# Rooms for the side jobs in a four-layer trunk: the operators' temporary gets its full size, the phases' tables leave the weight buffers

## The chip, the cores and the metric

One Trainium2 chip, one core in use. The metric is the device time of one execution in microseconds; of several runs the median counts. Profiles are of one execution.

## The reference

The model is a trunk of four layers on 512 tokens of width 1024, in f32. Each layer adds a mixer (S5, gated linear attention, differential attention, S5 again) and a feed-forward to the residual x:

```python
h = rmsnorm(x, norm_mix[layer])
x = x + mix(h)
h = rmsnorm(x, norm_ffn[layer])
g, u = split(h @ w_gate_up)            # 1024 -> 2 x 2816
x = x + (silu(g) * u) @ w_down         # 2816 -> 1024
```

The S5 mixer's recurrence over the sequence is linear with a constant complex diagonal: bb = f * b, p_j = exp(lr dt j) (cos(li dt j) + i sin(li dt j)), y = Re(c s) + d h. Its small operators (products of b, c and powers of the diagonal, and the cosine and sine of the phases) depend only on the weights of that layer, not on x.

## The kernel before

**Matmuls.** Products are f32 in three pieces: a weight tile is cast to a high part (ScalarE, L348) and a low part (VectorE, L356), and three matmuls (L376 to L378 for the down projection) add high by high, high by low and low by high. The gate and up products go by blocks of 256 hidden columns with seven products in place of eight (`seven_block`, matmuls of L543 into banks a, c, d), for which weight quarters are summed: by an accumulating DMA on POOL's queue (L579, "accum") and by VectorE (L636). Weight quarters sit in rotating slots ("slot", "halves", "gain", "side" are the names of such rooms). High and low parts share five buffers ("whl"), raw weights three ("wst").

**A pass.** A feed-forward has eleven blocks, in passes of 3, 3, 3, 2 in layer 0 and of 4, 4, 3 in the others. Behind a pass come its down products, `gemm_b`, for the left half of the output columns (d = 0) and then for the right (d = 1), each with four accumulator banks, one per 128 tokens; L526 adds a finished bank to x. The next half or the next block takes up a bank when L526 has read it.

**Jobs.** Beside the down products of two feed-forwards, `gemm_b` steps a generator once for each 128-row piece and token tile (`self.job()`, L403). What it yields comes between matmuls, so its vector and scalar work is placed there in each engine's own stream. In layer 0 the generator is `s5_spilled`: for the last layer's S5 it makes, in eight groups, the input operators X (`s5_x`), the output operators Q (`s5_q`), small transposes and maps (TensorE tiles xps, rps, cps), and stores them to DRAM ("in", "out", "map"). X is made by `cross`, a product pair with a temporary of tag "dx", Q by the same with the temporary "dq". X's last three powers need 192 elements of dx (L1070), the first needs 64. In layer 1 the generator is first the small tables of the attention, and then `s5_phases_spilled`: eight groups of angles, clamped, and their sine and cosine, each stored to DRAM as "cs".

**Rooms.** The jobs of layer 0 take their tiles from `Slices`, which hands out stretches of two large tiles one behind the other; the size of a tag's stretch is fixed by its first request, and a later, larger request of the tag starts at the same place. dx is first asked for with 64 elements, Q (tag "Q") is asked for next. In layer 1 each group of phases takes one whl buffer (8 KB a partition) for its angles g1 and its two tables cs. The names lie in the trace as "halves" (the rooms of layer 0's jobs) and "phases".

**Order.** Each engine runs its own instructions in the order of its stream, which a scheduler fixes when the kernel is built; between engines semaphores order what shares a room. DMAs issued on one queue go out in that order: SP's has the raw weights, POOL's the accumulating loads and all loads and stores of the jobs.

Of the kernel before, what the change touches and what calls it, by code (L numbers as in the profile page):

```python
# [11 lines left out]
F32 = mybir.dt.float32  # L12
# [3 lines left out]
AF = mybir.ActivationFunctionType  # L16
# [5 lines left out]
P = 128  # L22
# [246 lines left out]
class Trunk:  # L269
# [425 lines left out]
    def ffn(self, l, left, after=None, turn=False, aside=None, small=None):  # L695
# [7 lines left out]
        with self.tc.tile_pool(name=f"ffn{l}", bufs=1, reuse_waits="tile") as fp:  # L703

            na = 3 if aside else 4
            room = lambda: fp.tile([P, 2, 4, 256], F32, tag="act", name="lent", bufs=na)
# [5 lines left out]
            slots = [fp.tile([P, 4, 256], F32, name=f"slot{n}") for n in range(SLOTS + 2 * (4 - na))]  # L712
# [31 lines left out]
            for step in plan.split():  # L744
                name, _, n = step.partition(":")
# [18 lines left out]
            F = left.freed()  # L764
            if aside:

                self.jobs = aside(Slices(left.whole, left.g))
            else:

                self.jobs = small() if small else iter(())  # L770
                slots[:] = [F[0], F[1], slots[0], F[2], left.g[:].rearrange("p (k n) -> p k n", n=256), F[3]] + slots[1:]
            b0 = 0
            for nb in (4, 4, 3) if na == 4 else (3, 3, 3, 2):
                acts = []
                for n in range(b0, b0 + nb):
                    b = blocks[n]
# [450 lines left out]
            r = slice(g * 64, (g + 1) * 64)  # L1227
            self.nc.scalar.copy(d[r, :, :, r], ps[r])

    def s5_phases(self, pool, tag, L, kk, cs):  # L1230

        nc = self.nc
        v = nc.vector
        c = slice(L * NB + 4 * kk, L * NB + 4 * kk + 4)
        g1 = pool.tile([P, 4, P], F32, tag=tag, name="g")
        g2 = cs[:, 0].rearrange("p (b m) -> p b m", b=4)
        col = lambda k, b: self.k5[k][:, c.start + b : c.start + b + 1]
        for b in range(4):
            nc.scalar.activation(g2[:, b], self.mrow[:], AF.Identity, scale=col("f", b), bias=self.magic[:])
        yield  # L1240
        v.tensor_scalar_add(g2, g2, -MAGIC)
        yield
        for b in range(4):
            v.scalar_tensor_tensor(g1[:, b], self.mrow[:], col("fhi", b), g2[:, b], op0=ALU.mult, op1=ALU.subtract)
            v.scalar_tensor_tensor(g1[:, b], self.mrow[:], col("flo", b), g1[:, b], op0=ALU.mult, op1=ALU.add)
            yield
        v.tensor_scalar(g1, g1, -0.5, 0.5, op0=ALU.max, op1=ALU.min)
        yield
        ca = g1.rearrange("p b m -> p (b m)")
        nc.scalar.activation(cs[:, 1], ca, AF.Sin, scale=self.two_pi)  # L1250
        nc.scalar.activation(ca, ca, AF.Abs)
        nc.scalar.activation(cs[:, 0], ca, AF.Sin, scale=-self.two_pi, bias=self.halfpi[:])

    def s5_b_pads(self, bp, X, copies=False):
        for z in range(2):
# [6 lines left out]
    def s5_spilled(self, pool, L):  # L1262


        nc = self.nc
        inm = pool.tile([P, 2, 4, 64], F32, name="inmsp")
        mp = pool.tile([P, 4, 64], F32, name="mapsp")
        bp = pool.tile([P, 2, P], F32, name="bpsp")
        rs = pool.tile([P, 1, 112], F32, name="rssp")
        self.zero_off(bp, 16)  # L1270
        nc.gpsimd.memset(rs[:, :, :48], 0.0)
        self.spill = [{} for _ in range(8)]
        self.dq = nc.gpsimd
        raw = self.s5_loads(pool, L, 0, 4)

        def diag(dst, ps):
            for g in range(2):
                r = slice(g * 64, (g + 1) * 64)
                nc.scalar.copy(dst[r], ps[r, :, r])

        for kk in range(8):
            bb, craw = raw
            yield
            ps = self.s5_qt(craw)
            X, pre, one, two = self.s5_x(nc.vector, pool, L, 4 * kk, 4, bb)
            pre()
            one()
            yield
            yield
            two()  # L1290
            Q, base, one, two = self.s5_q(nc.vector, pool, L, 4 * kk, 4)
            base(ps)
            yield
            yield
            one()
            self.s5_b_pads(bp, X, True)
            yield
            yield
            two()
            if kk < 7:  # L1300
                raw = self.s5_loads(pool, L, 4 * kk + 4, 4)
            yield
            yield
            x0 = self.s5_xt(X, 0, 0)
            yield
            yield
            diag(inm[:, 0], x0)
            yield
            yield
            rv = self.s5_rows(4, bp, Q)  # L1310
            yield
            x1 = self.s5_xt(X, 1, 0)
            yield
            self.s5_map(L, 4 * kk, 4, rv, rs, mp, True)
            yield
            diag(inm[:, 1], x1)
            d = {w: self.dp.tile([P, n], F32, name=f"{w}{kk}") for w, n in (("in", 512), ("out", 512), ("map", 256))}
            nc.gpsimd.dma_start(d["in"][:], inm.rearrange("p a b c -> p (a b c)"))
            nc.gpsimd.dma_start(d["out"][:].rearrange("p (z b n) -> p z b n", z=2, b=4), Q[:, :, :, 1:5].rearrange("p z b j h -> p z b (j h)"))
            nc.gpsimd.dma_start(d["map"][:], mp.rearrange("p b n -> p (b n)"))  # L1320
            self.spill[kk].update(d)
            yield

    def s5_phases_spilled(self, L):

        for kk in range(8):
            p = Slices(self.wp.tile([P, 2048], F32, tag="whl", name="phases", bufs=5))
            cs = p.tile([P, 2, 512], F32, name="cssp")
            yield from self.s5_phases(p, "gsp", L, kk, cs)
            d = self.spill[kk]["cs"] = self.dp.tile([P, 1024], F32, name=f"cs{kk}")  # L1330
            self.nc.gpsimd.dma_start(d[:], cs.rearrange("p a b -> p (a b)"))
            for _ in range(4):
                yield

    def s5_in(self, p, xin, behind=()):
# [1113 lines left out]
```

## Time and profile before

| | |
|---|---|
| Median of 3 runs | 2328.56 us (2325.9 to 2330.97) |
| Span of the profiled execution | 2331.1 us |
| TensorE busy | 2227.3 us, 96% |
| VectorE busy | 1592.5 us, 68% |
| ScalarE busy | 1107.0 us, 47% |
| POOL busy | 276.6 us, 12% |
| Moved by DMA | 319.91 MB, mean 137 GB/s |

The profile's page gives no time of its execution but the span; it lies 0.1 above the slowest of the three runs and 2.5 above their median. A row of a timeline has the start in us, the duration, the engine, the line, the operation, what is written and read, and in brackets the idle time ahead of it with what ended that idle time. A row of waits has the sum, the number and the longest. Waits of an engine that is not the bound cost nothing by themselves. The granted clock of TensorE is a share of its full clock.

### The profile page before, as it was taken

The numbers are of one execution on the slowest core, as the hardware profiler recorded it, in microseconds if no ns is written. First come the engines' busy times: TensorE is split into PE (matmuls) and PEld (weight loads), VectorE is DVE, ScalarE is ACT, GpSimd is POOL, SyncE is SP. The second block draws the span as 40 slices with busy tenths as digits, with TensorE's granted clock in tenths as the row PEclk, the third lists the DMA queues.
The fourth block names the chain that finished last, engine by engine and source line by source line (L and its number), as shares of the span: only waits on it lengthen the run. The fifth ranks groups of instructions, "written<-read, shape, count | busy, mean of one in ns | idle before, by whom it ended". The sixth has DMA issues, their size and how long they took to land. (4 is left out here: it accounts for less than half of the span.)

```text
span 2331.1 us, 37161 instructions
## 1 busy us (share of the span) xinstructions
PE 2227.3 (96%) x14847; PEld 1975.7 (85%) x14847; DVE 1592.5 (68%) x2461; ACT 1107.0 (47%) x1769; POOL 276.6 (12%) x378
## 2 busy tenths in 40 slices
PE   5889989999999999999999998999999899999997
PEld 3778979898877799898988787989999788989996
DVE  8874877777624478786754676876766864967674
ACT  5533645454452355555534675653534233634342
POOL 1000132513000011110002131111000100101000
PEclk8899999999999999999999999999999999999999
DMA  4246566665322358675345465886641556766531
GB/s 85 40 125 180 140 156 161 157 171 135 109 89 73 115 140 204 166 170 168 86 146 128 108 132 144 207 215 146 164 117 54 133 150 151 191 172 159 159 81 64
DMA packets 295719, 319.91 MB, mean 137 GB/s; under 512 B 72125, under 2 KB 235225, under 8 KB 295290
## 3 DMA queue, kind: packets, MB, share of 16 engines
q1 hardware_dynamic: 233434, 236.31, 33.9%
q0 software_dynamic: 62112, 81.22, 18.7%
q8 instruction: 117, 1.92, 0.3%
q14 instruction: 56, 0.46, 0.1%
HBM read 285.62 MB, written 16.65 MB: 130 GB/s over the span
## 5 line engine op out<-in xcount | busy, mean ns | idle before, releaser
L356 DVE TENSOR_TENSOR whl<-wst,whl 128x1024 fp32r<-128x1024 f32 x272 | 331.3, 1223 | 255.1 <-ACT whl L348 254.6
L348 ACT CAST whl<-wst 128x1024 fp32r<-128x1024 f32 x272 | 284.3, 1051 | 319.0 <-PE acc L378 231.6
L543 PE MATMUL a<-side,whl 128*128 128x256 f32 x3168 | 384.0, 277 | 11.2 <-DVE whl L356 6.0
L543 PEld LDWEIGHTS a<-side,whl 128*128 128x128 f32 x3168 | 371.4, 188 | 13.0 <-DVE whl L356 6.8
L376 PE MATMUL acc<-whl,act 128*128 128x512 f32 x704 | 278.8, 396 | 0.0
L377 PE MATMUL acc<-whl,act 128*128 128x512 f32 x704 | 275.7, 392 | 0.0
L378 PE MATMUL acc<-whl,act 128*128 128x512 f32 x704 | 275.4, 391 | 0.0
L543 PE MATMUL c<-side,whl 128*128 128x256 f32 x2112 | 254.7, 277 | 2.9 <-DVE whl L356 2.9
L543 PEld LDWEIGHTS c<-side,whl 128*128 128x128 f32 x2112 | 247.2, 188 | 3.7 <-DVE whl L356 3.7
L356 DVE TENSOR_TENSOR whl<-slot,whl 128x1024 fp32r<-128x1024 f32 x105 | 127.9, 1223 | 68.5 <-ACT whl L348 68.4
L376 PEld LDWEIGHTS acc<-whl,act 128*128 128x128 f32 x704 | 132.7, 188 | 29.2 <-issue 1.2
L378 PEld LDWEIGHTS acc<-whl,act 128*128 128x128 f32 x704 | 132.7, 189 | 28.1
L377 PEld LDWEIGHTS acc<-whl,act 128*128 128x128 f32 x704 | 132.8, 189 | 26.1
L348 ACT CAST whl<-slot 128x1024 fp32r<-128x1024 f32 x105 | 110.1, 1054 | 80.5 <-PE acc L378 34.5
L376 PE MATMUL acc<-whl,hT 128*128 128x512 f32 x352 | 142.7, 405 | 2.1 <-DVE ro L2174 1.5
L543 PE MATMUL a<-sides,whl 128*128 128x256 f32 x1056 | 136.6, 286 | 2.7 <-DVE x L526 2.7
L377 PE MATMUL acc<-whl,hT 128*128 128x512 f32 x352 | 138.0, 392 | 0.9 <-DVE whl L356 0.9
L378 PE MATMUL acc<-whl,hT 128*128 128x512 f32 x352 | 138.2, 393 | 0.0
L543 PE MATMUL d<-sides,whl 128*128 128x256 f32 x1056 | 134.0, 283 | 1.5 <-ACT whl L348 1.5
L543 PEld LDWEIGHTS a<-sides,whl 128*128 128x128 f32 x1056 | 131.8, 194 | 3.9 <-issue 3.1
L543 PEld LDWEIGHTS d<-sides,whl 128*128 128x128 f32 x1056 | 129.1, 191 | 2.4 <-ACT whl L348 2.4
L682 ACT CAST act<-r 128x512 fp32r<-128x512 f32 (+1 forms) x110 | 66.3, 645 | 116.4 <-DVE r L661 102.9
(448 smaller groups left out, 3905.0 us busy)
## 6 DMA issues: line engine op xcount, KB each, us to landing
wst<-in_ffn_w_gate_up_dram SPq DMA_DIRECT2D x88, 512.0 KB, 4.6
wst<-in_ffn_w_down_dram SPq DMA_DIRECT2D x88, 512.0 KB, 4.5
slot<-in_ffn_w_gate_up_dram SPq DMA_DIRECT2D x69, 512.0 KB, 6.4
wst<-in_ffn_w_gate_up_dram POOLq DMA_DIRECT2D x44, 512.0 KB, 6.1
halves<-in_ffn_w_gate_up_dram SPq DMA_DIRECT2D x42, 512.0 KB, 5.4
wst<-in_s_w_glu_dram SPq DMA_DIRECT2D x32, 512.0 KB, 4.6
wst<-in_gla_w_in_dram SPq DMA_DIRECT2D x24, 512.0 KB, 3.9
wst<-in_diff_w_qkv_dram SPq DMA_DIRECT2D x24, 512.0 KB, 3.7
```

What stands on the lines that cost most here:

```text
L348: self.last["high"] = self.nc.scalar.copy(hl[:, 0], w[:])
L356: self.last["low"] = self.nc.vector.tensor_tensor(hl[:, 1], w[:], hl[:, 0].bitcast(F32), op=ALU.subtract)
L376: mm(out, lh, rh, start=first, stop=False)
L377: mm(out, lh, rl, start=False, stop=False)
L378: self.last["mm"] = mm(out, ll, rh, start=False, stop=last)
L543: mm(o, hl[:, x, k, c], side[:, y, k], start=first and not (j or k or n), stop=k == 3 and n == 2, skip_group_check=True,)
L682: self.last["act high"] = nc.scalar.copy(dst[:, 0, j], src[:, j])
```

## The change

Three edits:

- `s5_spilled` asks for dx once with [P, 4, 3, 16], its largest size, ahead of everything that comes behind it, so later requests of dx lie in 192 elements of their own.
- `s5_phases` takes its angles from a room that is handed in, and its two tables as two separate tiles. The angles lie in the norm's gain tile of the feed-forward (1024 elements a partition, two rooms of 512, group by group in turn). The tables are two tiles of 512 from the pool of normed rows, tag "hh" for even groups, "h" for odd ones, each with two buffers: so the tables of a group take the rooms of the group before the last. The gain tile was one of the rotating weight slots of that feed-forward and is none in layer 1 now: seven slots in place of eight. In layers 2 and 3 nothing changes.
- A group's tables are stored by two DMAs of 256 KB in place of one of 512 KB, and seven turns lie behind a group in place of four.

```diff
--- before.py
+++ after.py
@@ -767,8 +767,11 @@
                 self.jobs = aside(Slices(left.whole, left.g))
             else:
 
-                self.jobs = small() if small else iter(())
-                slots[:] = [F[0], F[1], slots[0], F[2], left.g[:].rearrange("p (k n) -> p k n", n=256), F[3]] + slots[1:]
+                spare = left.g[:].rearrange("p (k n) -> p k n", n=256)
+                slots[:] = [F[0], F[1], slots[0], F[2], *(() if small else (spare,)), F[3]] + slots[1:]
+                if small:
+                    self.turns = left.g[:].rearrange("p (z n) -> p z n", z=2)
+                    self.jobs = small()
             b0 = 0
             for nb in (4, 4, 3) if na == 4 else (3, 3, 3, 2):
                 acts = []
@@ -1227,13 +1230,13 @@
             r = slice(g * 64, (g + 1) * 64)
             self.nc.scalar.copy(d[r, :, :, r], ps[r])
 
-    def s5_phases(self, pool, tag, L, kk, cs):
+    def s5_phases(self, room, L, kk, cs):
 
         nc = self.nc
         v = nc.vector
         c = slice(L * NB + 4 * kk, L * NB + 4 * kk + 4)
-        g1 = pool.tile([P, 4, P], F32, tag=tag, name="g")
-        g2 = cs[:, 0].rearrange("p (b m) -> p b m", b=4)
+        g1 = room.rearrange("p (b m) -> p b m", b=4)
+        g2 = cs[0].rearrange("p (b m) -> p b m", b=4)
         col = lambda k, b: self.k5[k][:, c.start + b : c.start + b + 1]
         for b in range(4):
             nc.scalar.activation(g2[:, b], self.mrow[:], AF.Identity, scale=col("f", b), bias=self.magic[:])
@@ -1247,9 +1250,9 @@
         v.tensor_scalar(g1, g1, -0.5, 0.5, op0=ALU.max, op1=ALU.min)
         yield
         ca = g1.rearrange("p b m -> p (b m)")
-        nc.scalar.activation(cs[:, 1], ca, AF.Sin, scale=self.two_pi)
+        nc.scalar.activation(cs[1], ca, AF.Sin, scale=self.two_pi)
         nc.scalar.activation(ca, ca, AF.Abs)
-        nc.scalar.activation(cs[:, 0], ca, AF.Sin, scale=-self.two_pi, bias=self.halfpi[:])
+        nc.scalar.activation(cs[0], ca, AF.Sin, scale=-self.two_pi, bias=self.halfpi[:])
 
     def s5_b_pads(self, bp, X, copies=False):
         for z in range(2):
@@ -1270,6 +1273,7 @@
         self.zero_off(bp, 16)
         nc.gpsimd.memset(rs[:, :, :48], 0.0)
         self.spill = [{} for _ in range(8)]
+        pool.tile([P, 4, 3, 16], F32, tag="dx", name="dx")
         self.dq = nc.gpsimd
         raw = self.s5_loads(pool, L, 0, 4)
 
@@ -1324,12 +1328,13 @@
     def s5_phases_spilled(self, L):
 
         for kk in range(8):
-            p = Slices(self.wp.tile([P, 2048], F32, tag="whl", name="phases", bufs=5))
-            cs = p.tile([P, 2, 512], F32, name="cssp")
-            yield from self.s5_phases(p, "gsp", L, kk, cs)
+            tag = "h" if kk % 2 else "hh"
+            cs = [self.np_.tile([P, 512], F32, tag=tag, name="cssp", bufs=2)[:] for _ in range(2)]
+            yield from self.s5_phases(self.turns[:, kk % 2], L, kk, cs)
             d = self.spill[kk]["cs"] = self.dp.tile([P, 1024], F32, name=f"cs{kk}")
-            self.nc.gpsimd.dma_start(d[:], cs.rearrange("p a b -> p (a b)"))
-            for _ in range(4):
+            for z in range(2):
+                self.nc.gpsimd.dma_start(d[:, z * 512 : (z + 1) * 512], cs[z])
+            for _ in range(7):
                 yield
 
     def s5_in(self, p, xin, behind=()):
```

Lines from L773 on move by three to five in the changed kernel: L1070 is L1073 there, L1239 is L1242, L1247 is L1250, L1252 is L1255, L1318 and L1319 are L1322 and L1323.

The first place is on VectorE in layer 0, pass 1, at the turn from the first half of the down products to the second (banks acc_2752 to acc_2755). The rows "128x192" of L1070 write dx. Before:

```order
L1069 TENSOR_TENSOR halves_1541<-halves_1541,pw_131 128x4x48
L526 SCALAR_TENSOR_TENSOR x_1537<-acc_2752,rcol_1544,x_1537 128x512
L526 SCALAR_TENSOR_TENSOR x_1537<-acc_2753,rcol_1544,x_1537 128x512
L526 SCALAR_TENSOR_TENSOR x_1537<-acc_2754,rcol_1544,x_1537 128x512
L526 SCALAR_TENSOR_TENSOR x_1537<-acc_2755,rcol_1544,x_1537 128x512
L1070 TENSOR_TENSOR halves_1541<-halves_1541,pw_131 128x192
L1071 TENSOR_TENSOR halves_1541<-halves_1541 128x4x48
L1070 TENSOR_TENSOR halves_1541<-halves_1541,pw_131 128x192
L1071 TENSOR_TENSOR halves_1541<-halves_1541 128x4x48
```

And with the change:

```order
L1073 TENSOR_TENSOR halves_1541<-halves_1541,pw_131 128x192
L1074 TENSOR_TENSOR halves_1541<-halves_1541 128x4x48
L1073 TENSOR_TENSOR halves_1541<-halves_1541,pw_131 128x192
L356 TENSOR_TENSOR whl_3182<-wst_3172,whl_3182 128x1024
L526 SCALAR_TENSOR_TENSOR x_1537<-acc_2752,rcol_1544,x_1537 128x512
L1074 TENSOR_TENSOR halves_1541<-halves_1541 128x4x48
L526 SCALAR_TENSOR_TENSOR x_1537<-acc_2753,rcol_1544,x_1537 128x512
L526 SCALAR_TENSOR_TENSOR x_1537<-acc_2754,rcol_1544,x_1537 128x512
L1072 TENSOR_TENSOR halves_1541<-halves_1541,pw_131 128x4x64
L1073 TENSOR_TENSOR halves_1541<-halves_1541,pw_131 128x256
L526 SCALAR_TENSOR_TENSOR x_1537<-acc_2755,rcol_1544,x_1537 128x512
```

The two products that write dx stand ahead of the four L526 now, and products of Q (128x256, 128x4x64) between the last of them.

The second place is POOL's queue at the same time. in0 and out0 are the stores of the first group, rd1_0 one of its small rows, wst_3178 the accumulating load. Before:

```order
L579 DMA wst_3178<-in_ffn_w_gate_up_dram 128x4x256
L1318 DMA in0_2907<-halves_1541 128x512
L1319 DMA out0_2908<-halves_1541 1024x1x64
L1187 DMA rd1_0_2892<-halves_1541 128x112
L1079 DMA halves_1541<-in_s5_b_im_dram 128x4x16
L1082 DMA halves_1541<-in_s5_c_re_dram 128x64
L1082 DMA halves_1541<-in_s5_c_im_dram 128x64
```

And with the change:

```order
L1082 DMA halves_1541<-in_s5_b_im_dram 128x4x16
L1082 DMA halves_1541<-in_s5_b_re_dram 128x4x16
L1323 DMA out0_2908<-halves_1541 1024x1x64
L1190 DMA rd1_0_2892<-halves_1541 128x112
L1322 DMA in0_2907<-halves_1541 128x512
L1082 DMA halves_1541<-in_s5_b_re_dram 128x4x16
L1082 DMA halves_1541<-in_s5_b_im_dram 128x4x16
```

The store out0 is issued ahead of the loads of the next group, and the accumulating load (L579), which stood in front of it, comes later.

The third place is layer 1, pass 1, the same turn of the down products: ScalarE first. whl_8685 and its like are weights, phases_8576 and cssp_8576 the tables of the first group of phases, phases_8705 and cssp_8732 those of the third. Before:

```order
L1252 ACTIVATE phases_8576<-phases_8576,halfpi_117 128x512
L348 CAST whl_8690<-wst_8688 128x1024
L1250 ACTIVATE phases_8634<-phases_8634 128x512
L1251 ACTIVATE phases_8634<-phases_8634 128x512
L1252 ACTIVATE phases_8634<-phases_8634,halfpi_117 128x512
L1239 ACTIVATE phases_8705<-mrow_232,magic_123,s5f_128 128x128 x4
L348 CAST whl_8731<-wst_8729 128x1024
```

And with the change:

```order
L1253 ACTIVATE cssp_8577<-gain_6967 128x512
L1254 ACTIVATE gain_6967<-gain_6967 128x512
L348 CAST whl_8723<-wst_8721 128x1024
L1255 ACTIVATE cssp_8576<-gain_6967,halfpi_117 128x512
L1242 ACTIVATE cssp_8732<-mrow_232,magic_123,s5f_128 128x128 x4
L348 CAST whl_8768<-wst_8766 128x1024
L1253 ACTIVATE cssp_8646<-gain_6967 128x512
```

The first pieces of the third group stand right behind the last table of the first group now, whose room they write, and a weight's cast behind them; before, a cast and the second group's tables stood between.

VectorE at this turn, acc_8459 to acc_8462 being the banks of the first half. Before:

```order
L356 TENSOR_TENSOR whl_8685<-wst_8683,whl_8685 128x1024
L1247 TENSOR_SCALAR phases_8634<-phases_8634 128x512
L356 TENSOR_TENSOR whl_8690<-wst_8688,whl_8690 128x1024
L526 SCALAR_TENSOR_TENSOR x_1537<-acc_8459,rcol_7149,x_1537 128x512
L526 SCALAR_TENSOR_TENSOR x_1537<-acc_8460,rcol_7149,x_1537 128x512
L526 SCALAR_TENSOR_TENSOR x_1537<-acc_8461,rcol_7149,x_1537 128x512
L526 SCALAR_TENSOR_TENSOR x_1537<-acc_8462,rcol_7149,x_1537 128x512
L1241 TENSOR_SCALAR phases_8705<-phases_8705 128x512
L356 TENSOR_TENSOR whl_8731<-wst_8729,whl_8731 128x1024
```

And with the change:

```order
L1248 SCALAR_TENSOR_TENSOR gain_6967<-mrow_232,s5flo_130,gain_6967 128x128
L1244 TENSOR_SCALAR cssp_8732<-cssp_8732 128x512
L1250 TENSOR_SCALAR gain_6967<-gain_6967 128x512
L1247 SCALAR_TENSOR_TENSOR gain_6967<-mrow_232,s5fhi_129,cssp_8732 128x128 x2
L1248 SCALAR_TENSOR_TENSOR gain_6967<-mrow_232,s5flo_130,gain_6967 128x128 x2
L526 SCALAR_TENSOR_TENSOR x_1537<-acc_8459,rcol_7149,x_1537 128x512
L526 SCALAR_TENSOR_TENSOR x_1537<-acc_8460,rcol_7149,x_1537 128x512
L526 SCALAR_TENSOR_TENSOR x_1537<-acc_8461,rcol_7149,x_1537 128x512
L526 SCALAR_TENSOR_TENSOR x_1537<-acc_8462,rcol_7149,x_1537 128x512
L1247 SCALAR_TENSOR_TENSOR gain_6967<-mrow_232,s5fhi_129,cssp_8732 128x128 x2
L1248 SCALAR_TENSOR_TENSOR gain_6967<-mrow_232,s5flo_130,gain_6967 128x128 x2
L356 TENSOR_TENSOR whl_8768<-wst_8766,whl_8768 128x1024
```

Six instructions on the third group's tables and angles, and the clamp of the second group, stand ahead of the four L526 now; before, the third group began behind them.

## The prediction

> **What bounds the kernel now.** I read the page's busy table first, then the busy times by stretch, then what TensorE waited for, and last the timelines of the engines that it waited for.
>
> ```profile
> PE 2227.3 (96%) x14847; PEld 1975.7 (85%) x14847; DVE 1592.5 (68%) x2461; ACT 1107.0 (47%) x1769; POOL 276.6 (12%) x378
> ...
> 320.00:337.00 17.00, 11.37 (x87) 8.42 (x87) 10.54 (x20) 4.49 (x12) 8.43 (x13) 0.95 0.66 163
> 337.00:345.00 8.00, 8.00 (x58) 5.92 (x56) 5.31 (x16) 3.47 (x10) 2.97 (x6) 0.67 0.49 81
> 430.00:435.00 5.00, 3.76 (x43) 2.74 (x43) 4.57 (x15) 3.13 (x9) 3.17 (x7) 1.00 0.68 181
> 870.00:880.00 10.00, 8.26 (x73) 8.07 (x72) 9.45 (x11) 6.08 (x7) 2.07 (x2) 1.00 1.10 295
> 945.00:968.00 23.00, 23.00 (x104) 18.99 (x102) 14.85 (x38) 11.60 (x20) 2.46 (x4) 1.00 0.56 165
> 968.00:980.00 12.00, 9.27 (x54) 8.95 (x53) 9.50 (x10) 3.78 (x5) 1.31 (x1) 0.72 0.57 131
> ```
>
> In each stretch the columns are its length, then busy time (and count) of PE, PEld, DVE, ACT and POOL, then the granted clock. TensorE is the bound: 96% of the span. So the change can only be worth what it does to the few places where TensorE stands still or runs slowly. It touches two stages: the feed-forward of layer 0 (243 to 620 us), which carries the operators' jobs, and that of layer 1 (850 to 1160 us), which carries the phases' jobs. Where they have no hole, as from 945 to 968, the clock is 1.00 and PE is full.
>
> **Layer 0.** The first hole is in 320 to 337, with a slow clock behind it.
>
> ```profile
> PE xps L1217 <- DVE halves L1071: 4.7, 1, 4.7
> PE rps L1171 <- DVE halves L1069: 1.2, 1, 1.2
> PE rps L1171 <- DVE halves L1071: 0.9, 1, 0.9
> ...
> 336.41 1.12 PE L1217 MATMUL xps<-ident,halves 64*64 64x64 f32 x16 [4.69 <-DVE halves L1071]
> ```
>
> These three waits are all that TensorE's list has for 300 to 620 us. The xps transposes stand in TensorE's stream ahead of the next down products, and wait for a vector product. That one, in turn:
>
> ```profile
> 326.98 2.81 DVE L526 SCALAR_TENSOR_TENSOR x<-acc,rcol,x 128x512 f32<-128x512 f32 x4 [1.60 <-PE acc L378]
> 334.50 0.36 DVE L1070 TENSOR_TENSOR halves<-halves,pw 128x192 f32<-128x192 f32 x1 [4.71 <-DMA out<-halves]
> 335.92 0.35 DVE L1071 TENSOR_TENSOR halves<-halves 128x192 f32<-128x192 f32 x1
> ...
> 323.58 1.31 POOL L579 DMA_DIRECT2D wst<-in_ffn_w_gate_up_dram  x1 [2.83 <-ACT halves L1279]
> 324.37 1.11 POOL L1318 DMA_DIRECT2D in<-halves  x1
> 324.94 1.45 POOL L1319 DMA_DIRECT2D out<-halves  x1
> ...
> out<-halves POOLq DMA_DIRECT2D x1, 256.0 KB, 9.5
> ```
>
> VectorE stood still for 4.71 us in front of L1070, whose output is the 192-element temporary dx, until the store of the previous group's Q had landed: issued at 324.94, plus 9.5, is 334.4. The store was slow because a 512 KB accumulating load (L579) was issued ahead of it on the same queue. A temporary has no reason to wait for that store, except that its room lies on Q's: the code's allocator gave dx 64 elements at its first request and hands out the same start for 192 later.
>
> **Layer 1.** Here the hole is at the turn from the down products of pass 1 to the next block:
>
> ```profile
> 971.08 5.46 PE L543 MATMUL a<-sides,whl 128*128 128x256 f32 x24 [2.73 <-DVE x L526]
> ...
> 966.31 1.22 DVE L356 TENSOR_TENSOR whl<-wst,whl 128x1024 fp32r<-128x1024 f32 x1 [1.64 <-ACT whl L348]
> 967.79 1.22 DVE L356 TENSOR_TENSOR whl<-slot,whl 128x1024 fp32r<-128x1024 f32 x1
> 969.04 1.23 DVE L636 TENSOR_TENSOR slot<-slot,slot 128x1024 f32<-128x1024 f32 x1
> 970.19 2.06 DVE L526 SCALAR_TENSOR_TENSOR x<-acc,rcol,x 128x512 f32<-128x512 f32 x3
> ...
> 965.23 1.05 ACT L348 CAST whl<-wst 128x1024 fp32r<-128x1024 f32 x1 [3.24 <-DMA cs<-phases]
> ...
> 956.41 0.55 POOL L1331 DMA_DIRECT2D cs<-phases  x1 [0.88 <-DVE phases L1244]
> ...
> DMA to landing us min/median/max: 2.9/4.3/8.8
> ```
>
> From the end: TensorE wants the accumulator bank that L526 empties; L526 is queued behind the pieces of three weights; the first of them waits for a cast; and the cast waited 3.24 us for a "whl" buffer that phases held until its store had landed (956.41 + 8.8 = 965.2, the longest of the eight stores). Then the clock falls to 0.72.
>
> **The change part by part.** *dx gets its room.* No instruction is added; the wait of L1070 goes. What is late next: the two 192-element products now stand ahead of the four L526, and out0 is issued ahead of the accumulating load instead of behind it, so the store should land before Q is rewritten. The gain is the 4.69 of idle time and the slow clock behind it: (1 - 0.67) x 8.00 = 2.6. Of the other two waits (0.9 and 1.2 us) the order brings the small matrix products in other places, some of them closer to their inputs: from none to all of 2.1, and I take 1.2. Layer 0: -(4.7 + 2.6 + 1.2) = -8.5, between -7.3 and -9.4 if the store is no longer waited for.
>
> *The phases leave the weight buffers.* All five whl buffers stay with the weights, so the cast at 965.23 needs only TensorE's release of its buffer. The idle 2.73 goes and (1 - 0.72) x 9.27 = 2.6 of slow clock: -5.3. The order has one more L356 and one more L636 ahead of that L526 than before (1.2 us each), but the work can start some 2 us earlier than 966.31; were it not to, 0 to 2.4 us would come back. I take 0.
>
> *gain is no slot.* Seven rotating slots instead of eight in layer 1. Layer 0 has five and its list above has no TensorE wait on a slot: 0. The one load of the norm's gain on SP that now waits for the last angles stands ahead of no block's first weights: 0.
>
> *Rooms of two, and two stores per group.* This is what the change adds: eight more stores, whose issue (0.55 us each on POOL) lies beside everything. But a table room is reused by the group after next, so the first ScalarE piece of group 2 waits until the second half of group 0 has landed. Before, its buffer came round in the same way, but the pieces stood behind the second group's tables, and their vector work behind L526. In the new order they come right behind group 0's last table, and they and their vector work stand ahead of the L526 of the first down half. Before:
>
> ```profile
> 939.49 0.72 ACT L1252 ACTIVATE phases<-phases,halfpi 128x512 f32<-128x512 f32 x1
> ...
> 940.51 0.58 POOL L1331 DMA_DIRECT2D cs<-phases  x1 [23.12 <-DVE phases L1245]
> ...
> 944.10 1.64 ACT L1239 ACTIVATE phases<-mrow,magic,s5f 128x128 f32<-128x128 f32 x4
> ...
> 944.59 2.79 DVE L526 SCALAR_TENSOR_TENSOR x<-acc,rcol,x 128x512 f32<-128x512 f32 x4 [1.09 <-PE acc L378]
> 947.29 0.42 DVE L1241 TENSOR_SCALAR phases<-phases 128x512 f32<-128x512 f32 x1
> 948.86 0.61 DVE L1244 SCALAR_TENSOR_TENSOR phases<-mrow,s5fhi,phases 128x128 f32<-128x128 f32 x2
> ...
> 946.43 0.39 PE L376 MATMUL acc<-whl,act 128*128 128x512 f32 x1
> ```
>
> With group 0 ready at the same time, its second half is issued at about 940.5. Landing takes 2.9 to 4.3 (the shortest and the median of the 512 KB stores; half the bytes, so rather the shorter): 943.4 to 944.8. Then four pieces on ScalarE (1.64): 945.0 to 946.4. Then on VectorE the shift and the clamp (0.42 each) and two pairs of products (0.61 each), 2.06 in rows and some 1.8 as they overlap: L526 starts at 946.8 to 948.2 instead of 944.59. TensorE takes up the bank 0.9 after L526 begins (971.08 less 970.19 above), so 947.7 to 949.1, and it wants it at 946.43: a new wait of 1.3 to 2.7 us. The bottom end is below that if the tables are written a little earlier than now: 0. I take 1.6. Whether the clock falls behind it:
>
> ```profile
> 877.70 5.50 PE L543 MATMUL a<-side,whl 128*128 128x256 f32 x46 [1.74 <-DVE whl L356]
> ```
>
> A wait of 1.74 left the clock at 1.00 (870 to 880 above), one of 2.73 took it to 0.72. So 1.6 costs itself alone, 2.7 would cost 5.3. In pass 2 the same handover (group 4 to group 6) lies about one microsecond later against TensorE's need, by the same steps 0 to 1.5; I take 0.4.
>
> The Trainium skill (TensorE: Matmul & The Clock Gate, What's actually happening) has the clock fall after an idle window of about 3.4 us. The trace disagrees in part, since 2.73 us was enough here. By the page's figure even the longest new wait would keep its clock, and the 2.6 us behind the hole at 968 would be no part of the gain: -9.2 in place of the sum below. The Trainium skill (DMA: Bandwidth & Descriptors, Anatomy of one DMA — SWDGE) gives a store a fixed 2.0 us and 436 KB per us beyond it, which speaks against cutting one in two; by it, 256 KB land in 2.6 us, an estimate, and the new wait would be 1.0.
>
> *Sum.* -8.5 - 5.3 + 1.6 + 0.4 = -11.8, say -12. The profiled span is 2331.1 us, so 2319.3 for a profile; it lies 2.5 above the median 2328.56 of the runs, and the same -12 from the median is 2316.6.
>
> **The rivals.**
>
> *The new wait eats layer 1's gain* (0.20). The halves land later than the median, behind loads on the same queue (the page's longest is 8.8), so that the wait reaches 2.7 with its clock loss: 5.3, as much as the hole at 968 was. For it: nothing stands between a table and the piece that needs its room again; against it: the first store is issued when no accumulating load is ahead of it. Time: -8.5 + 0.4, or 2320.5.
>
> *Layer 0's wait moves to Q* (0.10). Q itself must still wait for its store, and the product that writes it now stands between the L526. If out0 lands at 334 as before, 7.3 stay: -12 + 7.3, or 2323.9. Against it: the new issue order, out0 in front of the load.
>
> *Slower* (0.08). One mechanism: in both passes the table store of the previous pair is late by a queue position, ScalarE stands before the next weight's cast, VectorE before L526. At a landing of 8.8 from 940.5 ScalarE goes on at 949.3, L526 starts at 952.8, TensorE at 953.7: 7.3 of wait and 2.6 of clock, and in pass 2 some 6 and 2.6: 18.5, against 13.8 gained: +4.7, or 2333.3. It decides from landings of about 7 in both passes.
>
> *Nothing moves* (0.07). The stage ends with its weights' transfers, not with TensorE, and the holes fill elsewhere: 2328.6. Against it: PE is 23.00 of 23.00 and at clock 1.00 where no hole is, with the transfers at 0.56.
>
> **How the numbers follow.** The forecast has 0.55: 2316.6. A measurement of this kernel tells about 0.2% (4.7 us) from no change. Forecast and the first rival are faster by more than that; Layer 0's rival lies on the edge, half and half; so faster 0.79, same 0.13, slower 0.08. The range: best, all holes gone and no new wait (-14.7, 2313.9) and 2.5 for the spread of the runs: 2311; worst within it, Layer 0's rival with 2 more: 2326.
>
> **What would show it.** Right: in the changed profile no DVE wait on out in 320 to 340, clock 1.00 behind it, pass 1 of layer 0 done 8 us earlier; no wait for cs in front of a weight's cast, no hole at the turn of pass 1 in layer 1; a new TensorE wait on L526 of 1 to 3 us at the middle of its down products, with the ScalarE piece of L1242 waiting for a cs store ahead of it. Wrong: xps still waiting 4 us with Q's product or a weight ahead of it; the clock below 0.8 at the middle of layer 1's down products; a first block behind the down products that waits for a slot.

## The result, and the profile after

The changed kernel takes 2320.19 us (median of 5 runs, 2318.39 to 2322.22); the kernel before, beside it, 2330.17 (2325.9 to 2330.97). The ratio is 0.9966, 95% interval 0.9955 to 0.9977: 5.4 to 10.5 us less. The forecast was 2316.6 in a range of 2311 to 2326, 12 us less. The profiled execution has a span of 2318.5 us against 2331.1. The changed kernel's lies 1.7 below the 2320.19 us of the same execution; if the same 1.7 holds before (an estimate), the profile of before is of an execution of 2332.8 us, slower than all five runs beside it.

The page's busy table of the changed kernel, and stretches of it (length, busy and count of PE, PEld, DVE, ACT, POOL, then the granted clock):

```profile
PE 2224.7 (96%) x14847; PEld 1973.3 (85%) x14847; DVE 1589.4 (69%) x2461; ACT 1105.8 (48%) x1769; POOL 280.9 (12%) x386
...
300.00:330.00 30.00, 30.00 (x220) 23.65 (x219) 23.91 (x56) 14.59 (x32) 12.36 (x20) 1.00 0.74 212
330.00:345.00 15.00, 15.00 (x109) 11.33 (x110) 11.86 (x27) 5.78 (x16) 11.89 (x19) 1.00 0.71 138
957.00:970.00 13.00, 13.00 (x104) 12.61 (x104) 7.28 (x8) 5.65 (x7) 0.00 (x0) 1.00 0.50 157
1050.00:1062.00 12.00, 10.96 (x49) 8.78 (x48) 9.86 (x20) 8.37 (x15) 2.72 (x4) 1.00 0.84 263
```

Where layer 0 had 11.37 busy of 17.00 and a clock of 0.67 behind it, TensorE is full at 1.00. So is the turn of pass 1 in layer 1 (957 to 970). A new hole is in 1050 to 1062. What TensorE waited for, first in 300 to 620 us (the one row there), then in 840 to 1160:

```profile
PE rps L1174 <- DVE halves L1074: 0.3, 1, 0.3
...
PE a L543 <- DVE whl L356: 1.7, 1, 1.7
PE acc L376 <- DVE x L526: 1.0, 1, 1.0
PE c L543 <- DVE whl L356: 1.0, 1, 1.0
PE d L543 <- ACT whl L348: 0.4, 1, 0.4
```

The 4.7, 1.2 and 0.9 of layer 0 are 0.3 in all. In layer 1 the 2.7 on L526 is gone, and 1.0 on L526 has come. The rest was there before. VectorE and POOL at layer 0's place:

```profile
322.68 0.35 DVE L1073 TENSOR_TENSOR halves<-halves,pw 128x192 f32<-128x192 f32 x1
324.83 1.23 DVE L356 TENSOR_TENSOR whl<-wst,whl 128x1024 fp32r<-128x1024 f32 x1 [1.81 <-ACT whl L348]
325.98 0.75 DVE L526 SCALAR_TENSOR_TENSOR x<-acc,rcol,x 128x512 f32<-128x512 f32 x1
...
317.39 0.86 POOL L1323 DMA_DIRECT2D out<-halves  x1 [3.96 <-DVE halves L1073]
...
out<-halves POOLq DMA_DIRECT2D x1, 256.0 KB, 4.6
```

The product that writes dx runs without a wait, ahead of L526. out0 goes out at 317.39, in front of the accumulating load, and lands 4.6 us later (it was 9.5), before Q is written at 328.23. In the four profiles without the room of dx this store took 8.6 to 9.5 us, in the three of the changed kernel and the two of the room of dx alone 4.6 to 5.2.

To place the gain I divide each profiled execution by counted matmuls of TensorE: cuts lie behind the first 1408 (at 240 us in the first profile of before), 4280 (620), 5397 (850) and 7642 (1170), each at the start of the next matmul. The stretches are the first mixer, layer 0's feed-forward, layer 1's mixer, layer 1's feed-forward, and the rest. In us, for all kernels of this study:

| | first mixer | layer 0 ffn | layer 1 mixer | layer 1 ffn | rest |
|---|---|---|---|---|---|
| before | 240.0 | 380.1 | 230.0 | 320.0 | 1161.0 |
| before, again | 237.5 | 379.7 | 230.0 | 316.0 | 1162.0 |
| before, seven slots | 237.3 | 380.1 | 228.4 | 316.0 | 1160.2 |
| changed | 239.3 | 370.1 | 231.6 | 315.5 | 1162.0 |
| changed, again | 236.3 | 369.9 | 228.5 | 315.3 | 1161.1 |
| changed, third | 239.6 | 369.9 | 231.6 | 315.3 | 1162.2 |
| room of dx only | 240.9 | 369.7 | 230.0 | 315.0 | 1162.0 |
| room of dx only, again | 239.8 | 369.5 | 230.0 | 315.0 | 1162.8 |
| all but the room of dx | 238.2 | 379.1 | 230.0 | 315.7 | 1161.4 |
| four turns | 240.4 | 369.1 | 230.0 | 320.6 | 1164.2 |
| nine turns | 240.3 | 370.4 | 229.9 | 319.0 | 1161.7 |
| tables stored twice | 239.1 | 370.2 | 230.0 | 322.3 | 1161.3 |
| estimate in the spare room | 237.9 | 370.2 | 231.6 | 314.0 | 1163.4 |

Layer 0's column has two values, 379 to 380 without the room of dx and 369 to 370 with it. Layer 1's column says something the first two profiles alone did not: its 4.5 us of difference are mostly the first profile's own, since the kernel before has 316.0 in its second. The first column varies by 4.6 us between kernels that do the same there.

### The profile page after: what moved, and what is told of

It reads as the page before. It is cut to its first block, busy times and chain, and to the rows that moved or that the text cites. A ratio compares the mean times of both kernels' runs of the same rounds, so it can differ in the third digit from the quotient of the medians.

```text
span 2318.5 us, 37186 instructions
## 1 busy us (share of the span) xinstructions
PE 2224.7 (96%) x14847; PEld 1973.3 (85%) x14847; DVE 1589.4 (69%) x2461; ACT 1105.8 (48%) x1769; POOL 280.9 (12%) x386
## 5 line engine op out<-in xcount | busy, mean ns | idle before, releaser
L348 ACT CAST whl<-wst 128x1024 fp32r<-128x1024 f32 x272 | 284.0, 1050 | 319.1 <-PE acc L378 228.4
```

Source lines behind the costliest of these rows:

```text
L348: self.last["high"] = self.nc.scalar.copy(hl[:, 0], w[:])
```

## The experiments

**Each part alone.** The room of dx is one line in the kernel before:

```diff
         self.spill = [{} for _ in range(8)]
+        pool.tile([P, 4, 3, 16], F32, tag="dx", name="dx")
```

> Only the room of dx, nothing in layer 1. If the gains are separate (theory): TensorE's waits in 300 to 620 us fall from 6.8 us to below 0.5, the clock of the stretch behind stays at 1.00, layer 0 ends about 9.9 us earlier than before against layer 0's start, and layer 1 keeps its hole of about 2.7 us before L526 with the clock at about 0.72 behind it: a time 9 to 10 us below before, near 2320.5. Rival (the hole of layer 1 comes from where layer 0 leaves the queues, not from the phases' buffers): the hole goes too, and the time is 14 us or more below before.

Measured: 2321.78 us, median of 8 (2315.51 to 2324.94), ratio 0.9965 (0.9952 to 0.9978), the same as the whole change. TensorE's list for 243 to 620 us has none of the three waits any more. Its layer 1:

```profile
PE a L543 <- DVE x L526: 0.6, 1, 0.6
```

The hole at the turn of pass 1 is 0.6 instead of 2.7, though nothing of the phases was changed, and the slow clock behind it is gone. The expectation that layer 1 keeps its hole failed. By itself that speaks for the rival; the kernels below show how far. The other part alone is the change without its dx line:

```diff
         self.spill = [{} for _ in range(8)]
-        pool.tile([P, 4, 3, 16], F32, tag="dx", name="dx")
```

> All of the change but the room of dx. Theory: layer 0 keeps its 4.7 us wait of xps with the clock near 0.67 behind it; layer 1's hole at the turn of pass 1 goes (5.9 us) and a wait of about 1 us before L526 in the middle of pass 2's down products comes (1.3 us): 4 to 5 us below before, near 2325.6. Rival (the two parts need each other, the phases' stores being late because layer 0 shifts nothing): no gain, 2330.

Measured: 2327.01 us, median of 11 (2325.59 to 2331.45), ratio 0.9990 (0.9981 to 0.9998). The largest waits of TensorE between 243 and 1175 us:

```profile
PE xps L1220 <- DVE halves L1074: 4.2, 1, 4.2
PE a L543 <- DVE whl L356: 3.5, 2, 1.7
PE rps L1174 <- DVE halves L1072: 1.9, 1, 1.9
PE c L543 <- DVE whl L356: 1.9, 2, 0.9
PE acc L376 <- DVE x L526: 1.1, 1, 1.1
```

Layer 0 keeps its wait, layer 1 has the new one of 1.1, as the theory had it. The gain is smaller, 2.3 us (0.5 to 4.4) where 4 to 5 were expected, but clear of zero.

**The kernel before, once more.** No edit.

> The kernel before, once more, for a second profile. If the holes follow from the order of work (theory), xps waits 4.7 us within 0.3 and L526's hole in layer 1 is 2.7 within 0.5, each with a clock of 0.65 to 0.75 behind it. If they hang on how fast one store lands (rival), the sizes differ by more than a microsecond, or one is missing. The slow clock in layer 1's mixer (0.91 in 680 to 700) is expected anywhere between 0.8 and 1.0 by both.

One run, 2326.83 us. TensorE's waits in 243 to 620 us, then in 835 to 1175 us, then the landing of the eight table stores, then the cast ahead of the hole:

```profile
PE xps L1217 <- DVE halves L1071: 4.1, 1, 4.1
PE rps L1171 <- DVE halves L1069: 1.7, 1, 1.7
...
PE a L543 <- DVE x L526: 0.8, 1, 0.8
PE acc L376 <- DVE x L526: 0.6, 1, 0.6
...
DMA to landing us min/median/max: 2.9/4.1/7.3
...
960.32 1.06 ACT L348 CAST whl<-wst 128x1024 fp32r<-128x1024 f32 x1 [1.73 <-DMA cs<-phases]
```

Layer 0's wait follows from the order: 4.7, then 4.1, which is outside the 0.3 that the theory allowed, but the three waits there sum to 6.8 and 6.6. Layer 1's does not have a size of its own: 2.7, then 0.8. The cast waited 3.24 us for a table store in the first profile and 1.73 here. It is the third group's store both times, the longest of the eight: 8.8 us, then 7.3. So the rival was right for layer 1: the size of the hole depends on how fast this one store lands. The profile on which the forecast was made is the worst of five such kernels. In this one, the one below with seven slots and the two of the room of dx alone the same store is again the longest of the eight, with 7.3, 7.1, 7.6 and 7.3 us, and the holes are 0.8, 0.9, 0.6 and 0.5.

**The store, slowed.** To show that it is the store, the kernel with the room of dx alone writes each table twice:

```diff
             self.nc.gpsimd.dma_start(d[:], cs.rearrange("p a b -> p (a b)"))
+            d2 = self.dp.tile([P, 1024], F32, name=f"csb{kk}")
+            self.nc.gpsimd.dma_start(d2[:], cs.rearrange("p a b -> p (a b)"))
```

> The room of dx alone, with the phases in the weight buffers, and each group's tables stored twice, to two places in DRAM (the second store is extra work): a phases buffer is held until the second store has landed. If the hole at the turn of pass 1 is the landing of that store (theory), TensorE's wait on L526 there grows from 0.6 us (with the room of dx alone) to 2.5 us or more, with a clock of 0.65 to 0.8 behind it: layer 1 longer by 4 to 8 us, 2325 to 2330. If the hole comes of the vector work queued ahead of L526 (rival), it stays below 1 us and the time at 2321.

Measured: 2325.23 us, median of 10 (2322.48 to 2330.27), ratio 0.9988 (0.9979 to 0.9997). ScalarE, VectorE and TensorE at the turn, and the stretch's clock:

```profile
956.32 1.05 ACT L348 CAST whl<-wst 128x1024 fp32r<-128x1024 f32 x1 [3.77 <-DMA csb<-phases]
...
961.28 2.72 DVE L526 SCALAR_TENSOR_TENSOR x<-acc,rcol,x 128x512 f32<-128x512 f32 x4
...
962.17 4.52 PE L543 MATMUL a<-sides,whl 128*128 128x256 f32 x24 [4.63 <-DVE x L526]
...
957.00:970.00 13.00, 8.37 (x58) 7.98 (x57) 11.19 (x12) 5.38 (x8) 1.35 (x1) 0.87 0.52 116
```

The cast waits 3.77 us for the second store, and the hole grows from 0.6 to 4.63, layer 1 by 7.3 us (322.3 against 315.0), as expected. Not all of the 7.3 is this hole: 4.0 are, a second wait on L526 of 1.5 us at the turn of pass 2 is new, and most of the rest is slow clock. The chain from store to cast to L526 to TensorE is thereby shown, for all that its first size was a bad draw. The clock fell less than expected: 0.87 over this stretch, 0.72 over the one behind the first profile's smaller hole. The last section says why.

**Seven slots.** gain taken out of layer 1's slots and used for nothing, in the kernel before:

```diff
-                slots[:] = [F[0], F[1], slots[0], F[2], left.g[:].rearrange("p (k n) -> p k n", n=256), F[3]] + slots[1:]
+                slots[:] = [F[0], F[1], slots[0], F[2], *(() if small else (left.g[:].rearrange("p (k n) -> p k n", n=256),)), F[3]] + slots[1:]
```

> The kernel before with gain taken out of layer 1's rotating slots and used for nothing. If seven slots are enough (theory), no wait of TensorE in 850 to 1160 us comes of a weight's load, and layer 1's blocks start where they did within 0.5 us. If not, waits of L543 on L356 or L348 of 1 us or more appear in the blocks of passes 2 and 3.

One run, 2323.74 us. Layer 1 takes 316.0 us, as in the second profile of before, and its list has no row that was not there. The slot costs nothing that this profile shows, as forecast.

**The turns between groups.** Four and nine in place of seven:

```diff
-            for _ in range(7):
+            for _ in range(4):
                 yield
```

> The change with four turns behind a group instead of seven. If the turns matter (a group's room is reused sooner, so more of its pieces wait for a store in front of L526), layer 1 gains waits of TensorE of 1 to 4 us over the changed kernel, and the time is 1 to 6 us above it, 2321 to 2326. If the rooms alone do it, layer 1 is as long as in the changed kernel within 1 us, 2320.

Measured: 2325.53 us, median of 10 (2322.17 to 2330.36), ratio 0.9984 (0.9975 to 0.9993). Layer 1:

```profile
PE acc L376 <- DVE x L526: 2.1, 1, 2.1
PE a L543 <- DVE x L526: 2.0, 1, 2.0
...
957.00:970.00 13.00, 10.99 (x78) 10.58 (x77) 8.05 (x9) 4.18 (x6) 0.00 (x0) 0.87 0.59 151
```

Layer 1 is 5.2 us longer than in the changed kernel (320.6 against 315.3 to 315.5): the turns matter. Some 1.7 of the 5.2 are slow clock behind the hole at the turn of pass 1. With four, the moved rooms are worse than the weight buffers were.

```diff
-            for _ in range(7):
+            for _ in range(9):
                 yield
```

> The change with nine turns behind a group instead of seven, so that in pass 2 of layer 1 the pieces ahead of L526 are group 5's, whose rooms group 3's stores left long before. If the wait left in pass 2 is the handover of a table's room (theory), TensorE's 1.0 us wait on L526 there is gone and layer 1 is 1 to 1.3 us shorter than in the changed kernel; the time 2316 to 2320, not to be told from the changed kernel by runs alone. If the wait is VectorE's load of work ahead of L526 and not the store (rival), it stays at about 1 us or grows.

Measured: 2322.67 us, median of 6 (2319.62 to 2324.11), ratio 0.9972 (0.9961 to 0.9983). TensorE's waits in 835 to 1175 us that the changed kernel does not have in this form:

```profile
PE tp L115 <- DVE hh L93: 1.4, 1, 1.4
PE acc L376 <- DVE x L526: 1.3, 2, 1.1
PE acc L376 <- ACT cssp L1255: 1.0, 1, 1.0
```

Layer 1 is 3.6 us longer, not 1 shorter. The wait on L526 in pass 2 is down to 0.2 us, as the theory had it, but others have come: 1.0 behind ScalarE's L1255 at the middle of pass 1 (938 us), and at the end of layer 1 (1156 to 1159 us) 1.1 on L526 and 1.4 for the normed rows. The last group no longer ends within pass 2, and its tables come beside that end. Since the whole schedule moved, this kernel does not say by itself what made the wait in pass 2.

**The handover alone.** The rounded angle of a group is written to the other angle room instead of the group's table room. That room is free when ScalarE has done the group before; no store has to land.

```diff
-    def s5_phases(self, room, L, kk, cs):
+    def s5_phases(self, room, spare, L, kk, cs):
...
-        g2 = cs[0].rearrange("p (b m) -> p b m", b=4)
+        g2 = spare.rearrange("p (b m) -> p b m", b=4)
...
-            yield from self.s5_phases(self.turns[:, kk % 2], L, kk, cs)
+            yield from self.s5_phases(self.turns[:, kk % 2], self.turns[:, 1 - kk % 2], L, kk, cs)
```

> The change, with the first piece of a group (the rounded angle) written to the other angle room, not to the group's table room. So a group's start waits for the group before on ScalarE and for no store. If the wait left in pass 2 is the handover of a table's room (theory), TensorE's wait on L526 there (1.0, 0.7 and 1.1 us in three profiles) falls below 0.4 with no new one over 0.5 at the turns, and layer 1 is 0.5 to 1.3 us shorter than in the changed kernel; the time 2316 to 2320, within the noise of it. If VectorE's own load ahead of L526 makes it (rival), it stays at 0.7 to 1.5.

Measured: 2320.57 us, median of 5 (2318.68 to 2321.58), ratio 0.9965 (0.9952 to 0.9977). All of TensorE's waits in 835 to 1175 us:

```profile
PE a L543 <- DVE whl L356: 1.7, 1, 1.7
PE c L543 <- DVE whl L356: 0.9, 1, 0.9
PE d L543 <- ACT whl L348: 0.4, 1, 0.4
```

No wait on L526 is left, though as much vector work stands ahead of it, so that work is not what made the wait. Layer 1 takes 314.0 us in this one profile, the shortest of all, 1.3 to 1.5 less than in the changed kernel. So the new wait came of the handover of a table's room. In the runs the 1.3 us do not show.

It did not come of a store that lands late, as the theory had it. ScalarE and VectorE in the changed kernel ahead of the L526 in pass 2:

```profile
1052.11 0.50 ACT L1242 ACTIVATE cssp<-mrow,magic,s5f 128x128 f32<-128x128 f32 x1 [0.17 <-DMA cs<-cssp]
...
1054.93 0.43 DVE L1244 TENSOR_SCALAR cssp<-cssp 128x512 f32<-128x512 f32 x1 [2.10 <-ACT cssp L1242]
...
1058.63 2.72 DVE L526 SCALAR_TENSOR_TENSOR x<-acc,rcol,x 128x512 f32<-128x512 f32 x4
```

ScalarE waited 0.17 us for the store (0.27 in the third profile; in the second and without the room of dx nothing, with 0.7 and 1.1 us of wait on L526). But the group's four pieces stand between the tables of the group before, and VectorE stood still for 2.10 us until they were done. With the spare room they stand in one block and end 1.9 us earlier, counted from the start of layer 1. So the room costs by the order that it leads to when the kernel is built, more than by waiting for the store.

**The two together on one chip.** No edit: the kernel with the room of dx alone, and the changed one, again.

> The room of dx alone again, beside the changed kernel on one chip. If the phases' move is worth on the average what the first profile of before showed (5.9 less the new wait, some 4 us), this is 4 us above the changed kernel. If that hole was one execution's late store, as the second profile of before says (theory now), the two are within 2 us, and its profile shows a hole at the turn of pass 1 of between 0 and 1 us most of the time.

> The changed kernel a third time, beside the room of dx alone. Theory: within 2 us of it, 2317 to 2321; layer 1's turn of pass 1 without a hole, a wait of 0.5 to 1.3 us in pass 2. Rival: 4 us below it.

Measured: the room of dx alone 2318.94 us, median of 11 (2312.53 to 2327.64), ratio 0.9962 (0.9948 to 0.9976); the changed kernel 2319.71, median of 5 (2316.22 to 2320.65), ratio 0.9959 (0.9946 to 0.9972). Within 1 us, as the theory had it by then. The profiles agree: a hole of 0.5 us at the turn of pass 1 with the room of dx alone, none in the changed kernel, which has 1.1 in pass 2. A further set of the changed kernel:

> The changed kernel again, for a second profile and more times on the chip of its neighbours. If its layer 1 no longer hangs on how fast a store lands (theory), no hole of over 0.3 us at the turn of pass 1, a wait of 0.5 to 1.5 us in pass 2, layer 1 as long as in the first profile within 1 us, and a spread of the times no wider than 5 us; 2320. If it only had luck (rival), a hole of 0.5 us or more at the turn of pass 1.

2317.42 us, median of 6 (2312.69 to 2324.61), ratio 0.9956 (0.9941 to 0.9970). No hole at the turn of pass 1 in its profile, 0.7 on L526 in pass 2. Only the width of the times was missed: 12 us where at most 5 were expected. In layer 1 the three profiles agree (315.5, 315.3, 315.3), so that width is not from there.

## Why the prediction was right, and where not

**Layer 0, forecast -8.5: measured -9.9** (369.9 in the mean of the nine profiles with the room of dx, 379.8 in the mean of the four without; 380.1 to 370.1 in the pair of profiles). The step held in each of its parts: the wait was false sharing of a room with Q (two names on one room, of which one waits for the other without using its data), the slow clock behind it went with it, out0 went out ahead of the load, and Q did not take over the wait. The term was too small: of the two small waits I took 1.2 of 2.1, and the list has 0.3 left of all; and the slow clock began at 335.46, ahead of the stretch that I priced, and cost 2.9 in place of 2.6 (5.9 us of matmuls at half clock). That makes 9.4; the last half microsecond is not placed. The rival that the wait moves to Q is refuted: Q's product does wait for a store once in the changed profile, 1.4 us, with TensorE busy.

**Layer 1's hole, forecast -5.3: measured -1.7 in the mean of five profiles** (1.1 of hole and 0.6 of slow clock). The mechanism was right and shown by the doubled store; the size was one execution's. Five profiles of kernels that leave the phases in the weight buffers and store once have 2.7, 0.9, 0.8, 0.6 and 0.5 us, and a slow clock behind the first alone. The term was sized by one landing, 8.8 us, without a price for a faster one. The same store landed in 7.1 to 7.6 us in the other four: always the slowest of its eight, but 1.2 us or more earlier, and that was most of the hole. I did price the spread of the landing for the new wait, and not for the gain.

**The new wait in pass 1, forecast +1.6: measured 0.** The step that failed is "the first ScalarE piece of group 2 waits until the second half of group 0 has landed". ScalarE, VectorE and POOL in the changed kernel:

```profile
930.39 0.72 ACT L1255 ACTIVATE cssp<-gain,halfpi 128x512 f32<-128x512 f32 x1
931.92 1.65 ACT L1242 ACTIVATE cssp<-mrow,magic,s5f 128x128 f32<-128x128 f32 x4 [0.82 <-DMA cs<-cssp]
...
935.71 2.72 DVE L526 SCALAR_TENSOR_TENSOR x<-acc,rcol,x 128x512 f32<-128x512 f32 x4
...
929.18 0.60 POOL L1336 DMA_DIRECT2D cs<-cssp  x1 [16.46 <-DVE dtab L846]
931.40 0.57 POOL L1336 DMA_DIRECT2D cs<-cssp  x1 [1.63 <-ACT cssp L1255]
```

L1242 began at 931.92, half a microsecond after the second half was issued: it waited for the half issued at 929.18, by the semaphore in the trace, which landed at 931.90; the second landed at 935.84. The first of a group's tables is finished last, but here the tile of the next group that is written first took the room that came free first. So ScalarE waited 0.82 us, and L526 was in time. By the step as forecast it would have waited 3.9 us longer. Half of a group's tables could go early only because the store is cut in two, which the prediction had put among what the change adds. That half the bytes land rather sooner did not hold in general either: group 0's halves took 2.7 and 4.4 us, but all sixteen 2.3 to 6.1 with a median of 5.0, above the 4.3 of whole tables. Ahead of L526 stood five instructions on the third group and two on the second, not six and one as the text on the change has it.

**In pass 2, forecast +0.4: measured 1.0** of waiting (0.7 and 1.1 in the other profiles; 1.3 us against the spare room, by layer 1's column). It is inside the 0 to 1.5 given, but not by the steps given: ScalarE waited at most 0.27 us for a store there, and the wait came of where the pieces stand in its order.

**Together.** The forecast's -12 stood beside -12.6 in the pair of profiles, but in part by luck: -10 in layer 0 and -4.5 in layer 1, and +1.9 in places that the change does not touch. The -4.5 comes from the same profile of before that the forecast was made on, with its rare hole. Over all profiles it is -9.9 in layer 0 and -0.6 to -2.0 in layer 1 (the changed kernel's 315.4 against 316.0 of before outside its first profile, or 317.3 with it); the comparisons by runs give 0.9956 to 0.9966, some 8 to 10 us. Nearly all of it is the room of dx. The phases' part takes away a hole that is there with a random size and puts in a steady one of about 1 us. Alone it measured 0.9990 (0.9981 to 0.9998), 2.3 us; beside the room of dx no gain of it is seen (315.0 without it, 315.4 with it, and the same time by runs). The room of dx alone took 1.0 us off layer 1 (315.0 twice, against 316.0 in the second profile of before and with seven slots). So the two parts are not quite separate, though the prediction's sum has them so; why was not tried. The first rival, that the new wait eats layer 1's gain, came out near the truth in time, but not by its mechanism: there was little to eat. The prediction's chances add up to 0.80 for faster, 0.12 for same and 0.08 for slower by its own split, not 0.79 and 0.13.

Not settled: how often a hole as large as the first profile's 2.7 us comes, which sets what the phases' part is worth. Five profiles have it once.

## What to carry to other kernels

A store that a vector instruction waits for, where it does not need its data, is a sign of two names on one room: look for a temporary whose first request was smaller than a later one. Before pricing a hole, ask what ends it: one ended by a fixed order repeats (4.1 to 4.7 us in four profiles), the size of one ended by a single slow store is a draw (2.7 us once, 0.5 to 0.9 four times), and a second profile of the kernel before tells the two apart before anything is changed. A job that shares rooms with a store may do better to begin in a room that only engines free, and to write the stored room last: in one profile that took 1.3 us off layer 1, which the runs do not show.

## What was not expected of the hardware

The cost in clock behind a hole did not go by the hole's length, and the means over stretches hide how it goes. In narrow stretches the granted clock (third from the end) is 1.00 or 0.50 and nothing between. Four turns first, then the kernel before:

```profile
950.00:960.10 10.10, 8.09 (x38) 6.49 (x37) 8.68 (x17) 5.68 (x9) 2.56 (x3) 1.00 0.52 116
960.20:963.50 3.30, 3.30 (x18) 3.30 (x17) 2.40 (x3) 0.00 (x0) 0.00 (x0) 0.50 0.43 148
963.60:970.00 6.40, 6.40 (x57) 6.40 (x56) 2.45 (x2) 3.13 (x5) 0.00 (x0) 1.00 0.51 160
...
970.40:977.10 6.70, 6.02 (x28) 6.05 (x29) 5.91 (x7) 2.47 (x4) 1.31 (x1) 0.50 0.54 83
977.20:985.00 7.80, 7.80 (x67) 7.80 (x67) 3.32 (x3) 3.98 (x5) 1.31 (x1) 1.00 0.71 174
```

Wherever a slow stretch follows a hole named here, it lasts 3.41 or 6.83 us, and costs at most half of that. Behind holes of 2.0, 4.1, 4.3 and 4.63 us it was 3.41; behind 2.73, 4.2 and 4.69 it was 6.83; and the 2.15 us in pass 2 of the kernel with four turns left the clock at 1.00. Within a profile the slow stretches start whole multiples of 3.41 us apart (335.46, 687.03 and 970.34 in the first one: 103 and 83 times). Counted in windows of that raster, the 2.01 us hole lay in one window, and the 2.15 us hole was split over two, 1.71 and 0.44. A second slow window came where a hole reached 0.7 us or more into the first, and none where it reached 0.2 or less. The Trainium skill (TensorE: Matmul & The Clock Gate, What's actually happening) has a gate that counts in free-running windows of about 3.4 us. That the loss hangs on where a hole falls against the windows agrees with these rows, that a hole has to fill such a window does not. How much idle time is enough is not settled: 1.74 us within one window left the clock alone in layer 1 of the first profile, and in layer 0 holes of 1.74 and 1.48 us ahead of the small transposes (rps) of two others had a slow window behind them.

The clock also moved where TensorE was never idle, in layer 1's mixer: the changed kernel first, then its second profile.

```profile
670.00:690.00 20.00, 20.00 (x92) 17.01 (x91) 2.45 (x2) 2.99 (x5) 0.00 (x0) 0.83 0.25 75
...
660.00:680.00 20.00, 20.00 (x99) 15.97 (x98) 5.50 (x5) 9.33 (x14) 0.00 (x0) 1.00 0.35 105
```

That stage takes 228.4 to 231.6 us in the table, in steps of 1.6, whatever the kernel: it is 228.4 or 228.5 in the two profiles without a slow window there, 229.9 or 230.0 in the eight with one and 231.6 in the three with two. With the first mixer's 236.3 to 240.9 it makes 6.1 of the 7.5 us between the first and the second profile of the changed kernel. Whether it makes the 12 us between that kernel's fastest and slowest run too is not shown, since the slowest was not profiled. What sets it was not tried.
